# The third K quarter of an MLP's second product: plain instead of Strassen, with activations split as they are made

## The chip, the cores and the metric

The kernel runs on one core of a Trainium2 chip. The time is that of one execution on the device in microseconds (us); where several runs are given, their median counts. A core has a matrix engine (TensorE, PE in the rows; its weight loads are shown apart as PEld), a vector engine (DVE), a scalar engine (ACT), GpSimd (POOL, which here does little but issue DMAs that add to what is in their destination) and SyncE (SP, which issues the other DMAs). Each engine works through its own queue in order; semaphores tie the queues to each other. Matmuls write into PSUM, eight banks of 128 x 512 fp32; DVE and ACT take the results from there.

## What is computed

One layer of a diffusion backbone for 512 tokens of width 1024 with a context of 256 tokens. The change lies in its last part, the MLP:

```python
def mlp(s, shift, scale_m):
    hm = rms_norm(s, g_norm2) * (1.0 + scale_m) + shift
    return jnp.square(jax.nn.relu(hm @ w_mlp1)) @ w_mlp2

x_new = x.astype(jnp.float32) + gt1 * merge(y_attn, o_dl, dz, ga, gd)
x_new = x_new + gt2 * mlp(x_new, sh2, sc2)
```

`w_mlp1` is 1024 x 4096 and `w_mlp2` 4096 x 1024. What stands ahead of it (modulated norms, one wide projection, windowed attention, a gated delta rule in chunks, the branch projections) is the same before and after, but for the order in which its instructions are issued.

## The kernel before

**Numbers.** Every large product is made of three matmuls of a reduced fp32 format: an operand is split into a high part (a rounding copy on ACT, line 231) and a low part (the difference, on DVE, line 232; the helper `split` holds both), and high x high, high x low and low x high are summed in PSUM.

**The MLP by quarters.** The hidden width of 4096 is worked off in four quarters (`hf` 0 to 3) of 1024. In each quarter the first product makes `hb`, the squared activations, 1024 hidden rows by 512 tokens; the second product takes `hb` as the stationary operand and the quarter's rows of `w_mlp2` as the moving one. In quarter 0 the first product is plain (`wload` and `mm3`, lines 335 to 339). In the others the class `Pair` makes two blocks of 128 hidden rows at a time by Strassen's scheme with seven half-size products (line 1619, 128x256), four pairs a quarter. At a pair's end its sums go through Relu (line 1654) and Square (line 1656) on ACT into `hb`.

**The second product.** In quarters 0 to 2 the class `Down` does it by Strassen's scheme as well: seven products of half size in K, tokens and columns. Its activation sides are made from quarters of `hb` by `left` (sums on lines 1783 and 1786, then a split), its weight sides by DMAs that add one weight block to another in SBUF (line 1733, on POOL's queue) and a split. Matmuls are on lines 1807 to 1809. Each of the seven results has a running total over the quarters in SBUF, `accs_`: written by ACT in quarter 0, added to by DVE (line 1828) in quarters 1 and 2. In quarter 3 the class `Flat` does the product plainly: for each half `n` of the 1024 columns it holds four banks, one for each 128 tokens, and sums four pieces of K (256 rows each) into them (lines 1876 to 1878). Its `left` splits each piece of `hb` behind the pairs.

**The totals.** The generator `gather` turns the seven totals into the four blocks of the result: seven DMAs that add one total to another (line 1894), a gate row made by eight transposes (line 1898), four multiplications by the gate (line 1908), and eight DMAs that add the residual parked in the output tensor (line 1910). It advances among the pairs of quarter 3 (`GAT`). `Flat` then multiplies its own PSUM by the gate (line 1885), adds it (line 1887) and stores the result (line 1888).

**Loads for the next quarter.** `Down.run` starts the next quarter's first weights behind its fifth to seventh product (`LOADS`).

**What sets the order.** The code records all instructions first. `arrange` then issues them by a list scheduler with a cost model: on each engine the ready instruction with the lowest rank goes next. The rank is the place at which the code recorded it, changed by the table `SHIFTS`: an entry `(engine, first, end, places)` adds `places` to the rank of the recorded instructions `first` to `end` of that engine (0 PE, 1 DVE, 2 ACT; -1 all). So the table moves instructions on each engine, but the data they need stays the same. SBUF is one arena that is handed out in the order of recording; an instruction that writes a place again waits for the earlier readers.

Of the kernel before, what the change touches and what calls it, by code (L numbers as in the profile page):

```python
# [42 lines left out]
OUT = 4, 128, 1024  # L43
LAHEAD = 1
GAT = 0, 2
LOADS = (4, 5), (4, 5, 6)
P = 128
D = 1024
# [73 lines left out]
def tile_layer(ctx: ExitStack, tc: tile.TileContext, I: dict, out: bass.AP, dbg=None):  # L122
    nc = tc.nc
# [1450 lines left out]
    class Pair:  # L1574
# [67 lines left out]
        def second(self):  # L1642

            w, z = bank(), bank()
            o = self.o
            self.prod(w[:, :256], "12", "21")
            V.tensor_tensor(o[:, :256], self.u[:, :256], w[:, :256], op=ALU.add)
            w.free()
            self.u.free()
            self.prod(z[:, :256], "22", "T4")  # L1650
            self.prod(z[:, 256:], "S4", "22")
            V.tensor_tensor(o[:, 256:768], o[:, 256:768], z.ap, op=ALU.add)
            z.free()
            A.activation(o.ap, o.ap, AF.Relu)
            at = self.f % FT * 512
            A.activation(hb[:, at:at + 1024], o.ap, AF.Square)
            o.free()

    def combos():
# [175 lines left out]
    class Flat:  # L1835


        def __init__(self, hf):

            self.hf, self.src, self.parts = hf, I["wm2"][hf], []  # L1840
            self.made = self.pieces()
            self.ready = [next(self.made) for _ in range(2)]

# [9 lines left out]
                        split(e, hi, lo)  # L1853
                        yield [r32(b.rearrange("p (k c) -> p k c", k=2)) for b in (hi, lo)]

        def left(self):

            at = len(self.parts) * 1024
            bs = [alloc(1024), alloc(1024)]
            split(hb[:, at:at + 1024], *[b.ap for b in bs])  # L1860
            self.parts.append([r32(b.ap.rearrange("p (k t) -> p k t", k=2)) for b in bs])

        def run(self):

            self.ready.append(next(self.made))
            for n in range(2):
                z = [bank() for _ in range(4)]
                for p in range(4):
                    if len(self.parts) < 4:
                        self.left()  # L1870
                    hi, lo = self.parts[p]
                    wh, wl = self.ready.pop(0)
                    for tt, zz in enumerate(z):
                        c = slice(tt * P, tt * P + P)
                        for k in range(2):
                            PE.matmul(zz.ap, hi[:, k, c], wh[:, k], start=(p == k == 0), stop=False)  # L1876
                            PE.matmul(zz.ap, hi[:, k, c], wl[:, k], start=False, stop=False)  # L1877
                            PE.matmul(zz.ap, lo[:, k, c], wh[:, k], start=False, stop=(p == 3 and k == 1))  # L1878
                    m = next(self.made, None)
                    if m:  # L1880
                        self.ready.append(m)
                for tt, zz in enumerate(z):
                    cols, r = slice(n * 512, n * 512 + 512), tt % 2 * 512
                    y, t = alloc(512), ends[f"{1 + tt // 2}{1 + n}"][:, r:r + 512]
                    V.tensor_tensor(y.ap, zz.ap, grow[0][:, cols], op=ALU.mult)
                    zz.free()
                    V.tensor_tensor(t, t, y.ap, op=(ALU.add, ALU.subtract)[n])
                    nc.sync.dma_start(out=out[tt][:, cols], in_=t)
                    y.free()

    def gather():

# [21 lines left out]
            accs_.pop(w).free()  # L1914
        yield

    ends = {}
    grow = []
    FT = 8
    pairs = [[Pair(hf * FT + f) for f in range(0, FT, 2)] if hf else [] for hf in range(4)]  # L1920
# [3 lines left out]
    for hf in range(4):  # L1924
# [17 lines left out]
        if hf == 0:  # L1942
            for _ in late:
                pass
            scr_[0].free()
        ps_ = pairs[hf]
        for i, p_ in enumerate(ps_):
            p_.first()
            if i:
                p_.load2()  # L1950
            if i + 1 < len(ps_):
                p_.second()
            if i + 2 < len(ps_):
                ps_[i + 2].load1()
            if hf == 3 and i in GAT:
                next(last)
            if i == 2:
                down = (Flat if hf == 3 else Down)(hf)
                down.left()
        if hf:  # L1960
            ps_[-1].second()
        if hf == 3:
            for _ in last:
                pass
        down.run()
# [143 lines left out]
class Lists:  # L2109
# [177 lines left out]


SHIFTS = (
# [21 lines left out]
)  # L2311


# [120 lines left out]
```

## Time and profile before

| what | value |
|---|---|
| runs | 850.16, 851.46, 853.50 us, median 851.46 us |
| the profiled execution | 848.21 us |
| its span, from the first to the last instruction | 846.4 us |
| granted clock of TensorE | 0.999 of full speed |
| DMA moved | 127.31 MB, mean 150 GB/s |
| first Strassen product of the MLP's second product, on TensorE | from 556 us |
| last quarter's plain product, on TensorE | about 795 to 842 us |

Rows of groups read: line, engine, operation, what it writes and reads by the program's names (`m` is any buffer of the arena, `wh` and `wl` the high and low weights, `wr` raw weights), shape and count, then busy time in us, mean ns of one, and the engine's idle time just before, with what ended it. TensorE is the busiest engine by far in every stage; DVE comes next, and in the MLP it is busy for most of the time as well. Matmuls overlap in the pipeline, so the mean of one is longer than the step from one to the next.

### The profile page before, as it was taken

Reading aid. Unit: us, or ns where it says so; the run is one execution under the profiler, and the core shown is the slowest. Engines: PE = TensorE matmul, PEld = TensorE weight load, DVE = VectorE, ACT = ScalarE, POOL = GpSimd, SP = SyncE. Lnnn points to the kernel's source line nnn. Section 1 sums busy time; section 2 is a strip of 40 time slices with the busy share of each in tenths; the row PEclk is TensorE's granted clock in tenths of the full one; section 3 lists DMA queues with packets and bytes.
Section 4 is the critical chain, followed back from the end, with each engine's and each line's share of the span. In section 5 each row is a group of like instructions: output and inputs, shape, how many; then the busy total and the mean of one; then the engine's idle time right before and its main releaser. Section 6 shows DMA issues by size and latency. Waiting matters only on the chain.

```text
span 846.4 us, 18086 instructions
## 1 busy us (share of the span) xinstructions
PE 833.7 (98%) x7464; PEld 698.4 (83%) x7464; DVE 699.2 (83%) x1153; ACT 534.2 (63%) x920; POOL 60.3 (7%) x81
## 2 busy tenths in 40 slices
PE   8999999999999999999999999999999999999997
PEld 5688778887877778787778899888998899889986
DVE  5875999988779998868849879798689988989853
ACT  5568785487769896587754345398557447646520
POOL 0000011010000002000000000110011001111300
PEclk9999999999999999999999999999999999999999
DMA  9924365543221237643116755959259636998271
GB/s 367 369 76 100 76 151 124 124 85 70 38 38 31 62 116 243 213 141 103 41 41 246 241 161 190 312 131 264 95 157 194 169 129 162 187 269 229 35 190 50
DMA packets 38178, 127.31 MB, mean 150 GB/s; under 512 B 4688, under 2 KB 5200, under 8 KB 38096
## 3 DMA queue, kind: packets, MB, share of 16 engines
q1 hardware_dynamic: 30176, 99.43, 34.3%
q0 software_dynamic: 7920, 26.74, 18.6%
q8 instruction: 58, 0.95, 0.5%
q14 instruction: 24, 0.20, 0.1%
HBM read 118.29 MB, written 4.19 MB: 145 GB/s over the span
## 4 chain that ended last, share of the span: by engine, by line
PE 92%; DMA 5%; ACT 1%; DVE 1%; SPq 0%; issue 0%; ACTq 0%
PE banks L1619 14%; PE banks L1155 14%; PE banks L335 9%; PE banks L337 9%; PE banks L339 9%; PE banks L1809 4%; PE banks L1807 4%; PE banks L1808 4%; PE banks L1250 3%; PE banks L1201 3%; DMA m<-in_wada 2%; PE banks L732 2%; PE banks L1876 2%; PE banks L1878 2%; PE banks L1877 2%; DMA wr<-in_win 1%
## 5 line engine op out<-in xcount | busy, mean ns | idle before, releaser
L1619 PE MATMUL banks<-m,m 128*128 128x256 f32 x1008 | 126.2, 284 | 0.7 <-ACT m L231 0.7
L1619 PEld LDWEIGHTS banks<-m,m 128*128 128x128 f32 x1008 | 123.6, 192 | 2.9 <-ACT m L231 1.6
L231 ACT ACTIVATE m<-m 128x512 fp32r<-128x512 f32 (+2 forms) x123 | 90.9, 761 | 52.7 <-PE banks L1808 8.6
L232 DVE TENSOR_TENSOR m<-m,m 128x512 fp32r<-128x512 f32 (+2 forms) x123 | 103.0, 854 | 15.2 <-ACT m L231 12.9
L335 PE MATMUL banks<-m,wh 128*128 128x512 f32 (+1 forms) x312 | 112.1, 363 | 0.0
L337 PE MATMUL banks<-m,wh 128*128 128x512 f32 (+1 forms) x312 | 110.2, 355 | 0.0
L339 PE MATMUL banks<-m,wl 128*128 128x512 f32 (+1 forms) x312 | 109.6, 354 | 0.0
L1155 PE MATMUL banks<-m,wh 128*128 128x512 f32 x320 | 104.4, 401 | 1.3 <-ACT m L189 1.3
L299 ACT ACTIVATE wh<-wr 128x1024 fp32r<-128x1024 f32 (+1 forms) x60 | 56.6, 944 | 47.8 <-DMA wr<-in_wout 13.9
L1155 PEld LDWEIGHTS banks<-m,wh 128*128 128x128 f32 x320 | 59.2, 188 | 14.3 <-ACT m L189 1.8
L335 PEld LDWEIGHTS banks<-m,wh 128*128 128x128 f32 x312 | 58.9, 189 | 8.5 <-issue 0.5
L337 PEld LDWEIGHTS banks<-m,wh 128*128 128x128 f32 x312 | 59.0, 189 | 8.2 <-issue 0.5
L339 PEld LDWEIGHTS banks<-m,wl 128*128 128x128 f32 x312 | 58.9, 189 | 8.1 <-DVE wl L304 0.2
L1807 PE MATMUL banks<-wh,m 128*128 128x512 f32 x168 | 65.4, 392 | 0.0
L1808 PE MATMUL banks<-wl,m 128*128 128x512 f32 x168 | 65.2, 390 | 0.0
L1155 PE MATMUL banks<-m,wl 128*128 128x512 f32 x160 | 64.4, 404 | 0.4 <-DVE wl L304 0.4
L1809 PE MATMUL banks<-wh,m 128*128 128x512 f32 x168 | 64.4, 391 | 0.0
L304 DVE TENSOR_TENSOR wl<-wr,wh 128x1024 fp32r<-128x1024 f32 (+1 forms) x44 | 45.1, 1024 | 13.3 <-ACT wh L299 13.2
L335 PE MATMUL banks<-m,m 128*128 128x256 f32 (+1 forms) x136 | 45.6, 341 | 0.6 <-ACT m L344 0.5
L231 ACT ACTIVATE wh<-m 128x1024 fp32r<-128x1024 f32 x30 | 31.6, 1055 | 22.8 <-DMA m<-in_wm 15.5
L1733 POOL DMA_DIRECT2D m<-in_wm x24 | 20.8, 920 | 348.9 <-PE banks L339 167.2
L337 PE MATMUL banks<-m,m 128*128 128x256 f32 (+1 forms) x136 | 44.9, 337 | 0.1
(298 smaller groups left out, 1814.1 us busy)
## 6 DMA issues: line engine op xcount, KB each, us to landing
m<-in_wada SPq DMA_DIRECT2D x48, 512.0 KB, 5.0
wr<-in_win SPq DMA_DIRECT2D x38, 512.0 KB, 3.8
m<-in_wm SPq DMA_DIRECT2D x36, 512.0 KB, 4.9
wr<-in_wm SPq DMA_DIRECT2D x28, 512.0 KB, 4.5
m<-in_wm POOLq DMA_DIRECT2D x24, 512.0 KB, 7.6
wl<-in_win POOLq DMA_DIRECT2D x16, 512.0 KB, 6.0
m<-in_xT SPq DMA_DIRECT2D x8, 512.0 KB, 4.8
wr<-in_wbr SPq DMA_DIRECT2D x16, 256.0 KB, 2.6
```

The lines of the kernel that those rows point to most:

```text
L231: A.activation(r32(hi), src, AF.Copy)
L232: (eng or V).tensor_tensor(r32(lo), src, hi, op=ALU.subtract)
L299: upper[0] = A.activation(r32(hi), raw, AF.Copy)
L304: V.tensor_tensor(r32(lo), raw, hi, op=ALU.subtract)
L335: PE.matmul(acc, w[0][:, k, :], xhi, start=(start and i == 0), stop=False)
L337: r = PE.matmul(acc, w[0][:, k, :], xlo, start=False, stop=(end and w[1] is None))
L339: r = PE.matmul(acc, w[1][:, k, :], xhi, start=False, stop=end)
L1155: PE.matmul(acc.ap, w[x][:, k, :], hx[k][y], start=(k == p == 0), stop=(k == KT - 1 and p == 2))
L1619: PE.matmul(dst, r32(self.w[w][i][:, k * P:(k + 1) * P]), xs7[x][k][j], start=(n == 0), stop=(n == 11))
L1807: PE.matmul(zz, hi[:, kk, ts_], wh[:, k], start=(kk == 0), stop=False)
L1808: PE.matmul(zz, hi[:, kk, ts_], wl[:, k], start=False, stop=False)
L1809: PE.matmul(zz, lo[:, kk, ts_], wh[:, k], start=False, stop=(kk == 3))
```

## The change

The third quarter's second product becomes plain as well, so the class `Flat` now serves quarters 2 and 3 (`FLAT = 2`), and `Down` quarters 0 and 1. In those two quarters each pair splits its squares at once: Square in place, then the high copy into `hb` and the low part into a buffer of its own in the list `lows`; `Flat.left` is gone. At quarter 2 `hb` is given back and taken anew from the arena. `gather`, which needs the Strassen totals, now runs among the pairs of quarter 2, and `Flat` in quarter 2 adds its results to the gated blocks without storing them. `Flat.run` starts the next quarter's loads behind the first three K pieces of its second column half (`FLOADS`). The table `SHIFTS` is replaced by another of the same kind.

```diff
+FLAT = 2
+FLOADS = 4, 5, 6
...
             A.activation(o.ap, o.ap, AF.Relu)
             at = self.f % FT * 512
-            A.activation(hb[:, at:at + 1024], o.ap, AF.Square)
+            if self.f < FLAT * FT:
+                A.activation(hb[:, at:at + 1024], o.ap, AF.Square)
+            else:
+                A.activation(o.ap, o.ap, AF.Square)
+                lows.append(alloc(1024))
+                split(o.ap, hb[:, at:at + 1024], lows[-1].ap)
...
-            self.hf, self.src, self.parts = hf, I["wm2"][hf], []
+            self.hf, self.src = hf, I["wm2"][hf]
+            if hf < 3:
+                self.loads = [pairs[hf + 1][0].load1, pairs[hf + 1][0].load2, pairs[hf + 1][1].load1]
...
-        def left(self):
-
-            at = len(self.parts) * 1024
-            bs = [alloc(1024), alloc(1024)]
-            split(hb[:, at:at + 1024], *[b.ap for b in bs])
-            self.parts.append([r32(b.ap.rearrange("p (k t) -> p k t", k=2)) for b in bs])
...
-                    if len(self.parts) < 4:
-                        self.left()
-                    hi, lo = self.parts[p]
+                    hi, lo = (r32(ap.rearrange("p (k t) -> p k t", k=2)) for ap in (hb[:, p * 1024:p * 1024 + 1024], lows[p].ap))
...
+                    if n:
+                        lows[p].free()
+                    if self.hf < 3 and 4 * n + p in FLOADS:
+                        self.loads.pop(0)()
...
-                    nc.sync.dma_start(out=out[tt][:, cols], in_=t)
+                    if self.hf == 3:
+                        nc.sync.dma_start(out=out[tt][:, cols], in_=t)
...
+        if hf == FLAT:
+            hb.free()
+            hb = alloc(FT * 512, True)
...
-            if hf == 3 and i in GAT:
+            if hf == FLAT and i in GAT:
                 next(last)
             if i == 2:
-                down = (Flat if hf == 3 else Down)(hf)
-                down.left()
+                down = (Flat if hf >= FLAT else Down)(hf)
+                if hf < FLAT:
+                    down.left()
...
 SHIFTS = (
-    (-1, 3553, 4764, 98), (-1, 3512, 3594, 1006), (-1, 7403, 7446, -155), (-1, 1987, 1996, 101), (0, 2046, 2292, -17),
+    (0, 3509, 4763, 98), (0, 1987, 1996, 132), (0, 2046, 2346, -13), (-1, 6045, 6078, -107), (-1, 2025, 2189, -11),
```

In the order rows below, the line numbers of the changed kernel are two higher than before as far as line 1655; its plain product keeps lines 1876 to 1878. First TensorE where the third quarter's pairs end and its second product begins (`m_6546` and the like are pair operands, `m_8067` and `m_8068` the high and low of Strassen's first activation side). Before:

```order
L1619 MATMUL banks<-m_6546,m_8129 128x256 x2
L1619 MATMUL banks<-m_6546,m_8130 128x256
L1807 MATMUL banks<-wh_8058,m_8067 128x512
L1808 MATMUL banks<-wl_8059,m_8067 128x512
L1809 MATMUL banks<-wh_8058,m_8068 128x512
```

and of the change (`m_7698` is the new `hb`, `m_7793` the low half of its first piece):

```order
L1621 MATMUL banks<-m_6546,m_8158 128x256 x2
L1621 MATMUL banks<-m_6546,m_8159 128x256
L1876 MATMUL banks<-wh_8090,m_7698 128x512
L1877 MATMUL banks<-wl_8091,m_7698 128x512
L1878 MATMUL banks<-wh_8090,m_7793 128x512
```

The Strassen product's rows are replaced by the plain product's at the same place; 18 of the plain ones already stand further up among the pairs.

Second ACT at the last two pairs of that quarter (`m_7941`, `m_8071` before and `m_7955`, `m_8100` after are the pairs' sums, `m_6265` the old `hb`). Before:

```order
L1654 ACTIVATE m_7941<-m_7941 128x1024
L1656 ACTIVATE m_6265<-m_7941 128x1024
L231 ACTIVATE m_8067<-m_6265 128x1024
L231 ACTIVATE wh_8063<-m_8050 128x1024
L231 ACTIVATE m_8183<-m_8185 128x1024
L231 ACTIVATE wh_8179<-m_8052 128x1024
L1654 ACTIVATE m_8071<-m_8071 128x1024
L231 ACTIVATE wh_8202<-m_8054 128x1024
L1656 ACTIVATE m_6265<-m_8071 128x1024
```

and of the change:

```order
L1656 ACTIVATE m_7955<-m_7955 128x1024
L1661 ACTIVATE m_7955<-m_7955 128x1024
L1632 ACTIVATE m_8101<-banks 128x512
L233 ACTIVATE m_7698<-m_7955 128x1024
L233 ACTIVATE m_8427<-m_8379 128x512
L233 ACTIVATE m_8382<-m_8378 128x512
L233 ACTIVATE m_8423<-m_8378 128x512
L1656 ACTIVATE m_8100<-m_8100 128x1024
L1661 ACTIVATE m_8100<-m_8100 128x1024
L233 ACTIVATE wh_8242<-wr_8240 128x1024
L233 ACTIVATE m_7698<-m_8100 128x1024
```

The copies that made Strassen's sides (`m_8067`, `m_8183`) are gone; relu, square and the high copy of a pair stand close together, with a weight copy and the next quarter's pair operands between them.

Third TensorE in the attention part, at the last projection product ahead of a wait for ACT (`st_2604` is a set of softmax sums, `wh_2426` and `wh_2596` the weights of two projection blocks). Before:

```order
L722 MATMUL banks<-m_2725,m_562 128x512
L1155 MATMUL banks<-m_136,wh_2426 128x512
L1155 MATMUL banks<-m_136,wl_2427 128x512
L753 MATMUL banks<-c_ident,st_2604 128x128
L1155 MATMUL banks<-m_136,wh_2596 128x512 x2
```

and of the change:

```order
L724 MATMUL banks<-m_2725,m_562 128x512
L1157 MATMUL banks<-m_136,wh_2426 128x512
L1157 MATMUL banks<-m_136,wl_2427 128x512
L755 MATMUL banks<-c_ident,st_2604 128x128 x2
L1157 MATMUL banks<-m_136,wh_2596 128x512 x2
```

One of the set's transposes, which stood further up, has moved down to this place.

More of the change, by code (lines that the diff above doesn't have):

```diff
@@ L1887, in run @@
                     V.tensor_tensor(t, t, y.ap, op=(ALU.add, ALU.subtract)[n])
-                    nc.sync.dma_start(out=out[tt][:, cols], in_=t)
+                    if self.hf == 3:
+                        nc.sync.dma_start(out=out[tt][:, cols], in_=t)
                     y.free()
+            lows.clear()
     def gather():
@@ L1915, in gather @@
         yield
-    ends = {}
+    ends, lows = {}, []
     grow = []
@@ L1954, in tile_layer @@
                 ps_[i + 2].load1()
-            if hf == 3 and i in GAT:
+            if hf == FLAT and i in GAT:
                 next(last)
             if i == 2:
-                down = (Flat if hf == 3 else Down)(hf)
-                down.left()
+                down = (Flat if hf >= FLAT else Down)(hf)
+                if hf < FLAT:
+                    down.left()
         if hf:
             ps_[-1].second()
-        if hf == 3:
+        if hf == FLAT:
             for _ in last:
```

38 rows, old and new, of the table SHIFTS are left out of this document.

## The prediction

> **What bounds the kernel now.** I read the page's head and its chain first, then TensorE's own rate by windows, then what TensorE waited for.
>
> ```profile
> span 846.4 us, 18086 instructions
> PE 833.7 (98%) x7464; PEld 698.4 (83%) x7464; DVE 699.2 (83%) x1153; ACT 534.2 (63%) x920; POOL 60.3 (7%) x81
> ...
> PE 92%; DMA 5%; ACT 1%; DVE 1%; SPq 0%; issue 0%; ACTq 0%
> ```
>
> TensorE is busy for 98% of the span and is 92% of the chain that ended last. Busy time overlaps itself, since matmuls are pipelined, so I look at the step from one to the next. The first row is the pairs' group on the page (count, busy, mean ns, idle before). The columns of a window are its length, then busy time and count (x) of PE, weight loads, DVE, ACT, POOL, then clock and DMA.
>
> ```profile
> L1619 PE MATMUL banks<-m,m 128*128 128x256 f32 x1008 | 126.2, 284 | 0.7 <-ACT m L231 0.7
> ...
> 680.00:720.50 40.50, 40.50 (x328) 39.99 (x327) 35.38 (x55) 24.67 (x33) 3.48 (x4) 1.00 0.50 131
> 720.50:761.40 40.90, 40.90 (x202) 34.43 (x201) 38.29 (x39) 23.53 (x27) 6.93 (x8) 1.00 0.95 229
> 761.40:797.00 35.60, 35.60 (x293) 35.01 (x292) 33.65 (x53) 23.53 (x33) 2.61 (x3) 1.00 0.50 139
> ...
> 604.00:634.00 30.00, 30.00 (x252) 30.00 (x251) 26.07 (x40) 18.36 (x25) 1.72 (x2) 1.00 0.40 125
> ...
> 800.00:840.00 40.00, 40.00 (x178) 33.10 (x178) 19.83 (x25) 8.39 (x8) 4.41 (x5) 1.00 0.51 128
> ...
> 730.00:744.00 14.00, 14.00 (x64) 11.58 (x63) 14.00 (x14) 8.52 (x9) 2.59 (x3) 1.00 0.86 208
> ```
>
> The first three windows are, roughly, the third quarter's pairs, its Strassen product, and the fourth quarter's pairs. The window 800 to 840 holds nothing on TensorE but the plain product of the last quarter. A matmul lasts 0.39 us there (the row of line 1878 further down), so the 178 began within 40.39 us: **0.227 us a step**. In the Strassen product (730 to 744) it is 14.39 / 64 = 0.225, so one 128x512 matmul costs the same in either form. A pair's 128x256 matmuls last 0.284 us and step at 30.28 / 252 = 0.120 (604 to 634, only pairs). The clock is 1.00 throughout.
>
> ```profile
> PE banks L1155 <- ACT m L189: 1.3, 2, 0.7
> PE banks L276 <- ACT m L271: 1.2, 1, 1.2
> PE banks L237 <- DVE ones L202: 1.1, 1, 1.1
> PE banks L732 <- DVE m L747: 0.8, 1, 0.8
> PE banks L1619 <- ACT m L231: 0.7, 1, 0.7
> PE banks L256 <- ACT m L189: 0.6, 1, 0.6
> PE banks L335 <- ACT m L344: 0.5, 1, 0.5
> PE banks L1155 <- DVE wl L304: 0.4, 1, 0.4
> PE banks L256 <- DVE modS L286: 0.3, 1, 0.3
> PE banks L407 <- DVE m L406: 0.3, 1, 0.3
> PE banks L256 <- DMA m<-in_wada: 0.2, 1, 0.2
> PE banks L681 <- ACT m L189: 0.2, 1, 0.2
> ```
>
> This is all that TensorE waited for (total, times, longest): 7.6 us. Behind 440 us there is one wait alone, 0.7 us on line 1619, and it stands where the first quarter's product meets the second quarter's pairs, ahead of anything the change rewrites. The waits on lines 276, 237, 335, 407 and 256, 4.2 us, belong to the first 40 us; the other 2.7 us lie between. So **the MLP's time is TensorE's instruction stream and nothing else**.
>
> **The change, part by part.** *Matmuls.* The Strassen product issues 7 products x 2 pieces x 2 row tiles x 2 x 3 = 168 matmuls of 128x512; the plain one 2 column halves x 4 pieces x 4 row tiles x 2 x 3 = 192. The code fixes both counts, so 24 more at 0.227 us: **+5.4 us**, all of it on the path. The bounds are 24 x 0.225 = 5.4 from the neighbouring window and, if the matmuls somehow ran like the half-size ones, 24 x 0.120 = 2.9. I take 5.4, the row of the very code that is used again.
>
> The Trainium skill bears on this (TensorE: Matmul & The Clock Gate, "Back-to-back issue gap"): it puts a sustained stream of weight loads and 512-column matmuls at about 131 ns each, and by that the term would be an estimated 24 x 0.131 = 3.1 us. Both windows disagree with it by 70%. So the rule is only a rival, below.
>
> *Vector and scalar work.* Counted over the two orders, the third quarter loses 13 DVE instructions that write 128x1024 (6 weight splits, 3 activation splits, 4 Strassen sums) and the 7 additions of line 1828, and gains 8 + 8 of 128x512 (lines 1885, 1887).
>
> ```profile
> L231 ACT ACTIVATE wh<-m 128x1024 fp32r<-128x1024 f32 x30 | 31.6, 1055 | 22.8 <-DMA m<-in_wm 15.5
> ...
> L232 DVE TENSOR_TENSOR wl<-m,wh 128x1024 fp32r<-128x1024 f32 x30 | 36.6, 1219 | 4.0 <-ACT wh L231 3.8
> ...
> L1828 DVE TENSOR_TENSOR m<-m,banks 128x1024 f32<-128x1024 f32 x14 | 17.0, 1214 | 2.9 <-PE banks L1809 2.9
> ...
> L1885 DVE TENSOR_TENSOR m<-banks,m x8: 679/686/692, 816.8 to 841.7; 128x512 f32<-128x512 f32 x8
> ```
>
> That is -13 x 1.22 - 7 x 1.21 + 16 x 0.69 = -13 us of DVE (line 1887 taken as line 1885), and ACT loses nine copies of 1.06 us. POOL loses 8 accumulating loads; SP's count stays (4 fewer raw and 4 fewer direct loads for the Strassen product, 8 for the plain one). Value: **nothing**. All of it runs beside TensorE, which waits for none of it in this quarter; even the MLP's single wait would give only 0.7 us. Below nothing: DVE could get crowded where work moves *in*. Into the third quarter's pairs come 4 low halves and the 4 gate products of line 1908, 8 x 1.22 = 9.8 us, and about 3 us of Strassen preparation goes out: 35.4 + 9.8 - 3 = 42 us of DVE beside 40.5 us of pairs and the 18 plain matmuls that now stand among them (4.1 us). That fits by 2 us. The fourth quarter's pairs in 761 to 797 already have DVE at 33.65 of 35.6 with no wait. So I put 0 to +3 us on it and take 0.
>
> *The chain behind the last pair.* Relu, square, copy and low half now follow each other; in the third quarter only the fourth K piece of the plain product needs the last pair's. After the last pair's matmul 78 of that half's matmuls remain, 54 ahead of the fourth piece: 54 x 0.227 = 12.3 us. The chain takes DVE 0.69, ACT 3 x 1.06, DVE 1.22 and a weight copy between, about 6 us. It is hidden; without that cover it would cost up to 6 us once.
>
> *Totals behind the second quarter.* POOL's seven additions and eight loads move one quarter forward with their rank in the queue kept.
>
> ```profile
> L1910 POOL DMA_DIRECT2D m<-out x8: 867/2018/3163, 797.3 to 801.2; - x8
> ...
> DMA to landing us min/median/max: 4.1/8.5/12.2
> ```
>
> Now the last is issued at 801.2 and lands at most 12.2 us on, 813.4; the first use is 816.8 or later (line 1885's row). After the change line 1908 stands among the second and third pairs on DVE, earlier against the same use than now, when it comes at the pairs' end, so the margin of 3 us or more grows. Cost 0. The fourth quarter's DVE is freed of it, and nobody waited there.
>
> *The end.* Only the last rows count, since the output store itself is unchanged.
>
> ```profile
> 841.30 0.39 PE L1878 MATMUL banks<-wh,m 128*128 128x512 f32 x1
> 841.73 0.69 DVE L1885 TENSOR_TENSOR m<-banks,m 128x512 f32<-128x512 f32 x1 [2.66 <-PE banks L1878]
> 842.45 0.69 DVE L1887 TENSOR_TENSOR m<-m,m 128x512 f32<-128x512 f32 x1
> 843.17 0.33 SPq L1888 DMA_DIRECT2D out<-m  x1
> ```
>
> One multiply, one addition and one store follow the last matmul. In the new order the last row tile's own 12 matmuls (2.7 us) come alone behind the others, where it was 18; the tile ahead of it needs 2 x 0.69 = 1.4 us, so the tail stays at one tile's. Cost 0.
>
> *The new shifts* move rows all through the program, also in the 556 us ahead of the first Strassen product. Two in five of TensorE's rows there change place, but the changes between whole-array and part-array matmuls stay at 110, and POOL's and SP's queues keep their order. The larger wait on line 189 shows what that can bring:
>
> ```profile
> 264.32 0.39 PE L1155 MATMUL banks<-m,wl 128*128 128x512 f32 x1
> 264.55 0.27 PE L753 MATMUL banks<-c_ident,st 128*128 128x128 f32 x1
> 265.56 0.73 PE L1155 MATMUL banks<-m,wh 128*128 128x512 f32 x2 [0.74 <-ACT m L189]
> ```
>
> One more transpose now stands in front of the waiting matmul, which wins at most that transpose's 0.27 us; the waiting matmul itself still stands right behind the same product, whose bank ACT must read first. The rows at the other waits (lines 732, 681 and the other two of line 1155) keep the instruction that ends them. In the first 40 us some 128x32 matmuls of line 256 go about one microsecond ahead of ready work; one of them waited 0.3 us for line 286, which also moves ahead by two on DVE. I take 0 for the order, with bounds: at best the 2.7 us between 40 and 440 and the MLP's 0.7 us all go (-3.4), at worst about as much is made anew (+3).
>
> **Sum.** **+5.4 us**. The profiled execution took 848.21 us (its span 846.4 and 1.8 around it), which would become 853.6. The three runs' median is 851.46, 3.25 above that one execution, and I carry the same addition: **856.9 us**. Half a per cent, about what a measurement of this kernel can tell from no change, is 4.3 us: 847.2 to 855.7. The forecast lies outside by only 1.2 us.
>
> **Rivals.** *The new order pays it back (not slower).* One mechanism: shifted rows put ready matmuls of lines 1155 and 721 into the waits between 40 and 440 us. Price: up to 3.4 us, so 851.46 + 5.4 - 3.4 = 853.5 us. It decides from 5.4 - 4.3 = 1.1 us of recovered waiting on. For it: all of these waits have other matmuls of the same stage close by. Against it: at those places both orders look alike. To get *faster* by over 0.5% the order would have to win 9.7 us, more than the 7.6 us of all waits in the trace, so it must also shorten the small gaps that no wait is named for.
>
> *A fuller DVE turns into a wait in the third quarter's pairs.* Price up to 3 us, 859.9 us. For it: 42 us of work in 44.6. Against it: 95% in the fourth quarter now, with no wait.
>
> *The added matmuls step faster than those of today.* From rows the floor is the half-size step: 24 x 0.120 = 2.9, 851.46 + 2.9 = 854.4 us, no change by the bound. Against it: 0.225 and 0.227 in two windows with either product. The Trainium skill's sustained 131 ns, on the page named above, would be this case; the trace speaks against it.
>
> **How the numbers follow.** Forecast 0.54; order pays back 0.28; a new DVE wait 0.11; a faster step 0.03; the order wins far more 0.04. The forecast's own spread of some 2 us about 856.9 crosses 855.7: I count 0.07 of its 0.54 as "same" and all of the DVE case as slower. Slower 0.47 + 0.11 = 0.58; same 0.07 + 0.28 + 0.03 = 0.38; faster 0.04. The range takes in the payback case with its own spread and the DVE case: 851.5 to 860.
>
> **What would show it.** Right: the plain matmuls of both quarters at 0.227 us a step, 24 more, the third quarter's pairs and product 5 us longer together, no wait on TensorE there, and the first Strassen product starting at the same time as now. Wrong: that product starting over 1.1 us earlier (the order); a wait of line 1619 or 1876 for DVE or ACT in the third quarter (crowding); a wait of line 1887 for POOL's loads; or a last store later than 5 us behind the last matmul.

## The result, and the profile after

The change made the kernel **slower by 0.7%**. In the comparison that judges it, five runs of the changed kernel gave a median of 857.07 us (855.38 to 857.88) and five of the kernel before 852.54 us (850.16 to 854.05): ratio 1.0072, 95% interval 1.0053 to 1.0090. A second comparison, made with the experiments, gave 855.68 us against 849.54 us: 1.0062 (1.0045 to 1.0078). By these ratios the change costs 6.1 and 5.3 us; 5.4 us and 856.9 us had been forecast. The ratios are not the quotients of the medians beside them: those are 1.0053 (4.5 us) and 1.0072 (6.1 us), so the cost is known to about a microsecond.

A warning for whoever subtracts the two traces: the profiled execution of before took 848.21 us, 4.3 us less than the median of its five runs, while that of after took 857.07 us, its median exactly. The difference of the two traces is therefore 8.9 us, of which about 3 to 4 us are the choice of executions. All that follows uses several executions of each order.

The head and the chain of waits of after's page (busy us, share of the span, instructions):

```profile
span 855.3 us, 18102 instructions
PE 840.9 (98%) x7488; PEld 703.2 (82%) x7488; DVE 686.0 (80%) x1149; ACT 525.3 (61%) x911; POOL 53.4 (6%) x73
...
PE 84%; DMA 7%; DVE 6%; ACT 2%; issue 1%; SPq 0%; ACTq 0%; DVEq 0%
```

24 matmuls more, DVE 13 us less, ACT 9 us less and POOL 8 instructions less, as counted beforehand; TensorE is still busy for 98% and bounds the kernel. Its share of the chain is lower than before (84% for 92%), since the chain follows the three waits shown below (2.7 us in all) back through splits and loads for some 87 us; in a second trace of the same kernel, without these waits, it is 94%. So that share is no measure of lost time. The group of the plain product's first line, and the window of after that lies wholly in the third quarter's plain product (length, then busy and count of PE, weight loads, DVE, ACT, POOL, then clock, DMA share, GB/s):

```profile
L1876 PE MATMUL banks<-wh,m 128*128 128x512 f32 x128 | 49.9, 390 | 0.0
...
730.00:744.00 14.00, 14.00 (x63) 11.62 (x62) 10.88 (x14) 7.47 (x9) 0.00 (x0) 1.00 0.22 77
```

The line serves both quarters now (128 where it had 64), a matmul lasts 0.39 us as before and (14.00 + 0.39) / 63 = 0.228 us is the step. In the same window DMA's share fell from 0.86 to 0.22. None of that is worth time, since TensorE did not wait there before either.

What TensorE waited for in after, behind 440 us (total, times, longest; the other rows of this view lie ahead of the MLP):

```profile
PE banks L1621 <- ACT m L233: 1.5, 1, 1.5
...
PE banks L1814 <- ACT wh L233: 0.8, 1, 0.8
...
PE banks L341 <- DVE wl L306: 0.4, 1, 0.4
```

Two of these are new and stand where the third quarter begins and in its pairs, at 667 us (line 1814, among the last matmuls of the second quarter's Strassen product) and at 696 us (line 1621), where the forecast had none. The wait of before at 586 us is gone.

### The profile page after: what moved, and what is told of

The parts are those of the page before. It is cut to its first block, busy times and chain, and to the rows that moved or that the text cites. A ratio compares the mean times of both kernels' runs of the same rounds, so it can differ in the third digit from the quotient of the medians.

```text
span 855.3 us, 18102 instructions
## 1 busy us (share of the span) xinstructions
PE 840.9 (98%) x7488; PEld 703.2 (82%) x7488; DVE 686.0 (80%) x1149; ACT 525.3 (61%) x911; POOL 53.4 (6%) x73
## 4 chain that ended last, share of the span: by engine, by line
PE 84%; DMA 7%; DVE 6%; ACT 2%; issue 1%; SPq 0%; ACTq 0%; DVEq 0%
PE banks L1157 14%; PE banks L1621 13%; PE banks L337 8%; PE banks L339 8%; PE banks L341 7%; PE banks L1876 3%; PE banks L1877 3%; PE banks L1878 3%; PE banks L1252 3%; PE banks L1203 3%; DMA m<-in_wada 3%; PE banks L1815 2%; PE banks L1816 2%; PE banks L1814 2%; PE banks L734 2%; DMA wr<-in_win 1%
## 5 line engine op out<-in xcount | busy, mean ns | idle before, releaser
L233 ACT ACTIVATE m<-m 128x512 fp32r<-128x512 f32 (+2 forms) x120 | 87.4, 754 | 59.7 <-DVE m L1612 11.4
L234 DVE TENSOR_TENSOR m<-m,m 128x512 fp32r<-128x512 f32 (+2 forms) x120 | 98.8, 848 | 14.7 <-ACT m L233 12.6
L233 ACT ACTIVATE wh<-wr 128x1024 fp32r<-128x1024 f32 x24 | 25.4, 1057 | 42.3 <-PE banks L1878 31.0
L1876 PE MATMUL banks<-wh,m 128*128 128x512 f32 x128 | 49.9, 390 | 0.0
L1877 PE MATMUL banks<-wl,m 128*128 128x512 f32 x128 | 49.9, 389 | 0.0
L1878 PE MATMUL banks<-wh,m 128*128 128x512 f32 x128 | 49.8, 389 | 0.0
L337 PE MATMUL banks<-m,m 128*128 128x512 f32 (+1 forms) x136 | 45.6, 341 | 1.0 <-ACT m L301 0.7
L520 DVE SCALAR_TENSOR_TENSOR m<-m,m 128x1024 f32<-128x1024 f32 x32 | 39.0, 1222 | 9.3 <-DMA m<-in_wada 9.3
L339 PE MATMUL banks<-m,m 128*128 128x256 f32 (+1 forms) x136 | 45.5, 339 | 0.0
```

The source lines that it names most:

```text
L233: A.activation(r32(hi), src, AF.Copy)
L234: (eng or V).tensor_tensor(r32(lo), src, hi, op=ALU.subtract)
L337: PE.matmul(acc, w[0][:, k, :], xhi, start=(start and i == 0), stop=False)
L339: r = PE.matmul(acc, w[0][:, k, :], xlo, start=False, stop=(end and w[1] is None))
```

## Experiments

Each ratio is against the kernel before on the same chip. Stretches are read from the start of TensorE's rows in the traces: "MLP" is the time from the first matmul of the first Strassen product (of the MLP's second product) to the last matmul of all.

| run | time, us (median) | ratio (95%) | first Strassen product, us | MLP, us | waits behind 440 us |
|---|---|---|---|---|---|
| before, first trace | 852.54 | | 555.73 | 285.57 | 586 |
| before, second trace | 851.48 (one run) | | 556.99 | 287.59 | 587, 647, 651, 789 |
| after, first trace | 857.07 | 1.0072 (1.0053 to 1.0090) | 557.13 | 293.07 | 496, 667, 696 |
| after, second trace | 855.68 | 1.0062 (1.0045 to 1.0078) | 556.32 | 289.91 | none |
| early order of before | 854.40 | 1.0055 (1.0042 to 1.0068) | 556.52 | 289.89 | 496 |
| before with early order of after | 850.52 | 1.0011 (1.0001 to 1.0021) | 556.71 | 285.41 | 587 |
| 24 fewer, first half | 852.80 | 1.0035 (1.0016 to 1.0054) | 557.33 | 287.55 | 695, 712, 731, 733 |
| 12 fewer, first half | 852.72 | 1.0026 (1.0011 to 1.0042) | 556.82 | 289.18 | 695, 707 |
| 24 fewer, second half | 850.00 | 1.0007 (0.9995 to 1.0018) | 558.40 | 284.95 | 497, 777 |
| small totals | 855.16 | 1.0069 (1.0048 to 1.0090) | 557.29 | 290.28 | none |
| fourth quarter alone plain | 851.13 | 1.0015 (1.0003 to 1.0027) | 556.73 | 287.92 | 587, 769, 787, 789 |
| before with new order of the first quarters | 854.57 | 1.0050 (1.0031 to 1.0069) | 556.37 | 292.38 | five from 634 to 660, three later |

The last column says where a matmul followed the one before it over 0.25 us later than the usual step (the time in us; 587 is the wait of before at 586).

### Both kernels once more

No edit. The kernel before:

> The kernel before, unchanged, profiled a second time: its first profiled execution (848.21 us) lay 4.3 us below the median of its five runs, so single traces cannot simply be subtracted. If the spread is a matter of single executions at one and the same instruction order, the first Strassen product should start anywhere within about 1.5 us of 555.7 us here, and the 0.9 us stall near 586 us may or may not be there. If the early order is what the change costs at its start (+1.4 us at that point in the two first traces), this trace starts that product at 555.7 +- 0.3 us and every trace of the changed kernel at 557.1 +- 0.3.

The kernel after:

> The changed kernel, unchanged. Time against before: 1.0055 to 1.009 (+4.5 to +8 us). If the two new waits on TensorE (about 1.0 us at 667 us on line 1814, about 1.7 us at 696 us on line 1621) belong to the order, they stand in this trace too, at the same instructions and with 0.8 us or more each; if they were chance of the one execution, at least one is missing or under 0.3 us.

One order spreads: the first Strassen product started at 555.73 and at 556.99 us in the two traces of before, and at 557.13 and 556.32 us in those of after. The sharper form of the expectation (one fixed time for each order) fell at once. All waits that the second trace of after names, in the view's order:

```profile
PE banks L278 <- ACT m L273: 1.2, 1, 1.2
PE banks L1157 <- ACT m L191: 1.2, 2, 0.6
PE banks L239 <- DVE ones L204: 1.1, 1, 1.1
PE banks L734 <- DVE m L749: 0.8, 1, 0.8
PE banks L258 <- ACT m L191: 0.6, 1, 0.6
PE banks L337 <- ACT m L301: 0.4, 2, 0.3
PE banks L1157 <- DVE wl L306: 0.4, 1, 0.4
PE banks L258 <- DVE modS L288: 0.3, 1, 0.3
PE banks L258 <- DMA m<-in_wada: 0.3, 1, 0.3
PE banks L1013 <- issue: 0.2, 1, 0.2
PE banks L683 <- ACT m L191: 0.2, 1, 0.2
```

No row of lines 1621, 1814 or 1876: the two new waits of the first trace are not fixed parts of the new order. The quickest traces of both kernels can now be set side by side: MLP 285.57 and 289.91 us, **4.3 us** apart.

### The early order and the MLP apart

The changed kernel, with the entries of before in `SHIFTS` for what is recorded ahead of the MLP (indices under 5740) and its own behind:

```diff
-    (0, 3509, 4763, 98), (0, 1987, 1996, 132),
...
+    (-1, 3553, 4764, 98), (-1, 3512, 3594, 1006),
...
     (-1, 6045, 6078, -107), (1, 5742, 6785, -6835),
...
```

> The changed kernel's MLP (its last 1730 rows on TensorE as in the changed kernel) behind the order of before in everything ahead of the MLP (the first 3008 rows on TensorE as before). Theory C (the early order costs nothing by itself, the 1.4 us at the first Strassen product in the two first traces was chance of the two executions): first Strassen product between 555.5 and 557.3 us, time against before as the changed kernel's, 1.005 to 1.008. Rival (the new early order costs 0.7 to 1.4 us): 1.0045 to 1.006, first product at 555.7 to 556.5. Rival (the new early order gains 2 to 3 us, which the MLP eats): 1.009 to 1.010.

And the kernel before with the new entries under 5740 and its own behind:

> The other half: the MLP of before (last 1722 rows on TensorE) behind the early order of the changed kernel. Theory C: 0.999 to 1.0015 of before, as many matmuls as before. Rival (early order costs): 1.001 to 1.002. Rival (early order gains): 0.9965 to 0.998. Together with the run of the early order of before, the two ratios less one should add up to that of the whole change.

Both ratios, 1.0055 and 1.0011, lie in the range of the theory that the early order costs nothing and in that of its rival, so the two do not decide it. The two parts add up: 0.55% for the MLP and 0.11% for the early order make 0.66%, between the 0.72% and the 0.62% of the whole. So **the MLP costs 4.7 us (3.6 to 5.8) and the early order 0.9 us (0.1 to 1.8)**. The traces point the same way on the second: with the early order of before the first Strassen product starts at 555.73, 556.99, 556.73, 556.52 and 556.37 us, 556.5 on average; with the new one at 557.13, 556.32, 556.71, 557.29, 557.33, 558.40 and 556.82, 557.1 on average, which is 0.7 us more where one order alone spreads by 1.3 us. The early order gains nothing; that it costs something is barely shown, since no cost at all lies just outside the interval.

### 24 of the added matmuls taken out, twice

In `Flat.run`, for quarter 2, the product of the activations' low half and the weights' high half is left out for three of four K pieces, first in the first column half, with the ranks of all other instructions kept:

```diff
+                            if self.hf == 2 and n == 0 and p < 3:
...
+                                continue
                             PE.matmul(zz.ap, lo[:, k, c], wh[:, k], start=False, stop=(p == 3 and k == 1))
```

> The changed kernel with 24 of the 192 matmuls of the third quarter's plain product left out (low halves of the activations by high halves of the weights, first column half, first three K pieces), everything else and its order as in the changed kernel: as many matmuls as the Strassen product had. Theory A (each added matmul costs its full step): 24 x 0.227 = 5.4 us less than the changed kernel, so 0.9998 to 1.003 of before. Rival (they step at 0.131 us): 3.1 us less. Rival (the stage waits for operands, so that matmuls are cover): under 1.5 us less.

Only 0.27% went, 2.3 us, which is less than Theory A's 5.4 and its first rival's 3.1; in the traces the MLP got 289.91 - 287.55 = 2.4 us shorter. The rest came back as waits, which the waits of TensorE name, line 1881 being the low x high matmul here:

```profile
PE banks L1876 <- ACT m L233: 1.2, 1, 1.2
...
PE banks L1881 <- DVE m L234: 0.7, 1, 0.7
```

The gaps between matmuls there, less the usual step, are 1.4 and 0.9 us, and two smaller ones at 695 and 712 us 0.3 each, so 5.4 - 2.9 = 2.5 us is what the rows leave. The stretch in the timeline (start, us, engine, line, operation; in brackets the idle time before and what ended it), DVE, then ACT, then TensorE:

```profile
726.39 0.69 DVE L234 TENSOR_TENSOR m<-m,m 128x512 fp32r<-128x512 f32 x1 [1.90 <-ACT m L233]
727.00 0.68 DVE L1654 TENSOR_TENSOR m<-m,banks 128x512 f32<-128x512 f32 x1
...
732.79 1.22 DVE L234 TENSOR_TENSOR m<-m,m 128x1024 fp32r<-128x1024 f32 x1
```

```profile
725.72 1.15 ACT L233 ACTIVATE m<-m 128x512 fp32r<-128x512 f32 x2 [1.96 <-DMA m<-in_wm]
727.71 1.06 ACT L1656 ACTIVATE m<-m 128x1024 f32<-128x1024 f32 x1 [0.84 <-DVE m L1654]
...
731.52 1.04 ACT L233 ACTIVATE m<-m 128x1024 fp32r<-128x1024 f32 x1
```

```profile
731.00 0.39 PE L1877 MATMUL banks<-wl,m 128*128 128x512 f32 x1
732.62 0.50 PE L1876 MATMUL banks<-wh,m 128*128 128x512 f32 x1 [1.23 <-ACT m L233]
732.95 0.40 PE L1877 MATMUL banks<-wl,m 128*128 128x512 f32 x1
734.06 0.50 PE L1881 MATMUL banks<-wh,m 128*128 128x512 f32 x1 [0.72 <-DVE m L234]
```

This is the chain behind the last pair, whose last matmul ended at 724.1 us. Its addition on line 1654 began only at 727.00, since DVE, in order, stood before a split whose copy waited for a load (725.72 on ACT). Relu, square, the high copy (to 732.56) and the low half (to 734.01) follow, with two weight copies between. The fourth K piece starts when the high copy ends, and its low half's first matmul when the low half does. In the changed kernel 54 matmuls stand between the last pair's matmul and the fourth piece and cover this chain; here the trace has 32 (7.3 us; the next expectation counts 30). So the experiment removed cover and matmuls at once, and the second version leaves the cover whole (`n == 1` in place of `n == 0`):

> The changed kernel again with 24 matmuls of the third quarter's plain product left out (low halves of the activations by high halves of the weights, first three K pieces), but from the second column half. In the run of the first half 24 x 0.227 = 5.4 us of steps went and 2.3 us came back as two waits at 731 and 733 us, on the first matmuls of the fourth K piece. Theory A with the chain behind the last pair (Relu, square, copy, low half: 7 to 10 us from the last pair's matmul, hidden by 54 matmuls = 12.3 us in the changed kernel, by 30 = 6.9 us there): this time the 54 stand, so no wait on the fourth K piece and the full 5.4 us go: 0.999 to 1.002 of before. Rival (the third quarter is paced by something else, loads or copies of weights, so that matmuls there are partly cover): only about 3 us go, 1.002 to 1.005, with waits of 2 us in the second column half or the pairs behind it.

Now it is level with before, at 1.0007, and the MLP takes 284.95 us, 5.0 us less than after's quickest, with one gap of 0.45 us at 777 us (0.3 us of it in the row of TensorE's waits below). The issue order moved a little too, and two of the fourth quarter's loads went out 20 us earlier (59 us behind the third quarter's first pair matmul, where after's second trace has 79), but the third quarter's stretch runs at the steps alone. From its first pair matmul to its product's last, after's second trace has 238 matmuls of 128x512 and 344 of 128x256: 238 x 0.227 + 344 x 0.120 = 95.3 us, and it took 95.27. Here they are 214 and 344, 89.9 us, and it took 89.81. **The 24 matmuls are the MLP's cost**, 5.4 us of steps, and nothing paces the third quarter in their place as long as the chain is covered.

```profile
PE banks L1621 <- ACT m L233: 0.3, 1, 0.3
```

Between the two, 12 matmuls left out of the first half (the same edit with `and k == 0`):

> The changed kernel with 12 matmuls left out ahead of the fourth K piece in the third quarter's first column half (low halves of the activations by high halves of the weights, first of the two 128-row slices of the first three K pieces), so that 42 x 0.227 = 9.5 us of matmuls stand over the chain behind the last pair, between the 12.3 us of the changed kernel (no wait) and the 6.8 us of the run with 24 left out (2.3 us of waits). Theory A with the chain at 7 to 10 us: 2.7 us less than the changed kernel and a wait on the fourth K piece of 0 to 0.5 us, so 1.002 to 1.0045 of before. Rival (chain of 6 us as predicted, the waits with 24 left out came from late loads alone): no wait at all, same time.

1.0026, 0.36% below after's ratio of 1.0062 in another comparison. Its trace has no wait on the fourth K piece, so 9.5 us of cover were still enough, and 7.3 us were not. It has another wait, on line 1621 at 695 us, the one that after's first trace showed, and a smaller one at 707 us; without these two gaps, 1.5 and 0.4 us, its MLP is 289.18 - 1.9 = 287.3 us, 2.6 us less than after's quickest, where 12 steps are 2.7.

### The totals on 16 of their 1024 columns

That wait stands some 28 us behind the third quarter's first pair matmuls, while POOL's transfers of the totals, which the change moved here, are under way:

```diff
-            G.dma_start(out=accs_[x].ap, in_=accs_[y].ap, accum_op=ALU.add)
+            G.dma_start(out=accs_[x][:, :16], in_=accs_[y][:, :16], accum_op=ALU.add)
```

> The changed kernel with the seven accumulating transfers of the totals on 16 columns in place of their whole width (most of the totals' sum is left out), same instructions in the same order. Theory B (these transfers share the DMA engines with the third quarter's weight loads, which then land late): the waits at 667 us (line 1814) and 696 us (line 1621) shrink to under 0.3 us, the loads of line 1594 issued near 683 land in 3 to 5 us instead of 9 to 10, and the time falls by 1.5 to 2.7 us against the changed kernel. Rival (the waits come from the order of the loads alone): both waits stay, time within 0.7 us of the changed kernel.

The time did not move (1.0069); the fall of 1.5 to 2.7 us did not come. But the second trace of after had shown meanwhile that the waits need not be there, so this run could gain little. Its order is also not quite that of the changed kernel, which the expectation takes it to be: in the third quarter splits on ACT and DVE and one weight load stand in other places, and 13 plain matmuls in place of 18 stand among the pairs. What it does show is the loads. The DMA issues of two 512 KB loads of line 1594 (1592 before), from issue to landing in us (the median of the two), for before, after's first and second trace, the run with small totals, and that with 12 fewer matmuls:

```profile
m<-in_wm SPq DMA_DIRECT2D x2, 512.0 KB, 3.5
```

```profile
m<-in_wm SPq DMA_DIRECT2D x2, 512.0 KB, 9.4
```

```profile
m<-in_wm SPq DMA_DIRECT2D x2, 512.0 KB, 6.7
```

```profile
m<-in_wm SPq DMA_DIRECT2D x2, 512.0 KB, 5.0
```

```profile
m<-in_wm SPq DMA_DIRECT2D x2, 512.0 KB, 9.4
```

With the whole totals the loads take 6.7 to 9.4 us, with small ones 5.0. The 3.5 us of before are not quite the same thing: its two loads were issued 6.1 us apart, those of the others 1.3. The two traces that waited for over 1 us are those with 9.4; the other four with whole totals have 6.7 to 8.1. It holds in all seven traces with this third quarter, with the landing of the first of the two loads counted from the third quarter's first pair matmul (the 337th of 1008):

| trace | landing after that matmul, us | idle on line 1621 near 695 us, us |
|---|---|---|
| small totals | 19.1 | none |
| after, second | 19.6 | none |
| 24 fewer, second half | 20.1 | none |
| early order of before | 20.9 | none |
| 24 fewer, first half | 21.1 | 0.1 |
| 12 fewer | 22.5 | 1.3 |
| after, first | 23.0 | 1.5 |

How the load reaches TensorE, in after's first trace: ACT stood idle for it, DVE for ACT's copy, and a later copy on ACT then came too late for the matmul (timelines of ACT, DVE, ACT and TensorE).

```profile
691.73 1.15 ACT L233 ACTIVATE m<-m 128x512 fp32r<-128x512 f32 x2 [3.42 <-DMA m<-in_wm]
692.40 1.90 DVE L234 TENSOR_TENSOR m<-m,m 128x512 fp32r<-128x512 f32 x3 [1.30 <-ACT m L233]
...
697.11 1.06 ACT L233 ACTIVATE m<-m 128x1024 fp32r<-128x1024 f32 x1 [0.23 <-DVE m L1601]
```

```profile
698.22 0.98 PE L1621 MATMUL banks<-m,m 128*128 128x256 f32 x6 [1.54 <-ACT m L233]
```

So the loads are slower where the totals run beside them, and have some 21 us of slack; past it a wait of up to 1.5 us follows, in two of the six executions with whole totals (0.1 us in a third). In the kernel before, which moves the totals in its fourth quarter, two loads of line 1592 issued beside them at 749.9 and 766.3 us took 6.7 and 5.9 us; but one at 723.3, ahead of the first of these transfers (741.6 us), took 8.0, so loads can be slow without them as well. That the totals' volume is the cause of the slow loads rests on one run (5.0 us, at another order) against six; that it costs time was not seen directly, since the run that took it away is compared with a kernel that mostly does not wait. What makes one execution's loads slower than another's at one order stays open, and so does the wait at 667 us, which stands in after's first trace alone.

### What is left when the third quarter is Strassen's again

The changed code with `FLAT = 3` and the shifts of before: only the fourth quarter is plain, and its activations are split as they are made.

```diff
-FLAT = 2
+FLAT = 3
```

> The changed code with its plain quarters set to the fourth alone (third by the Strassen product again, totals in the fourth quarter) and the shifts of before: what is left of the change is that the fourth quarter's activations are split as they are made, in place. As many matmuls as before (7464). Theory A (the added matmuls are the whole cost): 0.999 to 1.0015. Rival (the split as made, on the way of the pairs, costs by itself): 1.002 or more, with a wait of line 1621 or 1876 on ACT or DVE in the fourth quarter.

1.0015 (1.0003 to 1.0027): nearly all of the cost is gone with the plain third quarter. The rest, 1.3 us (0.3 to 2.3), is at the edge of what Theory A allows, and the rival's sign is there in part, so what it comes from is not clear. The trace has 2.1 us of waits of the pairs on ACT:

```profile
PE banks L1621 <- ACT m L233: 2.1, 3, 1.1
```

One is the old one at 587 us, the others are in the fourth quarter, where ACT came to a weight copy whose load was late (1.06 us idle for it at 768.72 us) with the pair's copy queued behind.

### A piece of the new order in the kernel before

In all four traces with the MLP order of before, TensorE waits near 586 us, as here in the first trace of before; in none of the seven with the changed kernel's does it.

```profile
586.20 0.39 PE L1808 MATMUL banks<-wl,m 128*128 128x512 f32 x1
587.33 0.39 PE L1619 MATMUL banks<-m,m 128*128 128x256 f32 x1 [0.74 <-ACT m L231]
```

1.13 us lie between the two starts, 0.9 more than a step. To have that without the matmuls, the kernel before got the new entries of `SHIFTS` for the indices 5740 to 6200 alone:

```diff
-    (-1, 6044, 6077, -106), (1, 5748, 5839, -1941),
+    (-1, 6045, 6078, -107), (1, 5742, 6200, -6835), (-1, 6143, 6195, -21), (0, 5899, 5917, -49), (0, 5926, 6155, 22),
```

> The kernel before, with the changed kernel's order only between the first quarter's product and the middle of the second quarter's pairs (TensorE's first 3008 rows and its last 704 as before): no plain third quarter, no other part of the change. Theory D (the 0.7 to 1.0 us wait of the pairs on ACT near 586 us, in all four traces with the old order of the MLP and in none of the six with the new one, is a matter of the order, and its going paid back 0.9 us of the added 5.4): that wait is gone, 0.9985 to 0.9995 of before. Rival (it goes and something behind it takes the time): wait gone, 0.9995 to 1.001. Rival (chance): the wait is there.

The wait near 586 is gone, as in every trace with the new order at this place, so it belongs to the order. But the kernel is 0.5% slower than before, more than the rival had allowed. Among its waits are new ones where the new order meets the old, in the second quarter's Strassen product and pairs:

```profile
PE banks L1807 <- ACT wh L231: 1.2, 1, 1.2
...
PE banks L1809 <- DVE m L232: 0.8, 1, 0.8
...
PE banks L1808 <- DVE wl L232: 0.6, 2, 0.4
...
PE banks L1619 <- DVE m L232: 0.6, 2, 0.4
...
PE banks L1807 <- ACT m L231: 0.5, 1, 0.5
```

At the same matmul counts its MLP takes 292.38 us in this trace where 285.41 are possible; by the ratio a seam in the order costs 4.2 us (2.6 to 5.9), nearly as much as the change itself. No run beat the kernel before.

## Why the prediction was right, step by step

- **Matmuls, +5.4 us: right.** 24 more at the step of 0.227 to 0.228 us; without them the kernel is level with before. The third quarter's pairs and product were to get 5 us longer together: from the first pair matmul to the product's last it is 94.57 us before and 95.27 in after's second trace, but the stretch of before holds 42 matmuls of the fourth quarter's pairs, 5.0 us, so they got 5.7 us longer. The Trainium skill's sustained 131 ns (TensorE: Matmul & The Clock Gate, "Back-to-back issue gap") would make an estimated 3.1 us of it; the step in both plain products and the 5.0 us that the MLP lost without them speak against it at this kernel's number format.
- **Vector and scalar work, nothing: right.** 13 us of DVE and 9 us of ACT went, and the fourth quarter's pairs have much lighter DVE, for no gain. The crowding in the third quarter was rightly sized, at 42 of 44.6 us or 94%, though its window left out the pairs' first 14 us; it did not bind: in the second trace of after, DVE is busy for 53.20 of the 56 us around those pairs, 95%, with no wait there.

```profile
667.00:723.00 56.00, 56.00 (x409) 53.08 (x408) 53.20 (x75) 32.59 (x45) 12.30 (x14) 1.00 0.88 218
```

- **The chain behind the last pair, hidden: right, though mis-sized.** It had been put at 6 us. From the end of the last pair's matmul to the end of the low half it takes 7.2 us in the second trace of after (722.97 to 730.15) and 9.9 us with 24 fewer matmuls, where DVE stood before a late load. What it left out is the queue ahead of it on DVE, an engine that works in order. With 12.3 us of cover neither matters; with 7.3 us of cover the longer one left waits of 2.3 us.
- **Totals behind the second quarter, cost 0: the step that failed.** It asked whether the totals come in time for their use, and they do: in after's first trace the last transfer is issued at 718.5 us and lands at most 7.9 us on, and the first addition that needs one starts at 743.3. It did not ask whom their transfers hold up. In the row above the DMA share is 0.88, where the third quarter's pairs of before had 0.50, and the loads beside them take up to 9.4 us, where small totals leave 5.0. The price, as far as these transfers are the cause, is 1.3 to 1.5 us in two of six executions; so the sign "no wait on TensorE there" failed in the very trace shown with the result. A wait of the pairs on ACT in the third quarter was also the sign set for a crowded DVE; but ACT had idled 3.42 us for the load, and DVE 1.30 us for ACT's copy, so the late load began it.
- **The end, 0: right.** One multiply, one addition and the store follow the last matmul, at the same distance: the addition starts 1.15 us behind that matmul's start, as before.

```profile
850.20 0.39 PE L1878 MATMUL banks<-wh,m 128*128 128x512 f32 x1
850.63 0.69 DVE L1889 TENSOR_TENSOR m<-banks,m 128x512 f32<-128x512 f32 x1 [1.30 <-PE banks L1878]
851.35 0.69 DVE L1891 TENSOR_TENSOR m<-m,m 128x512 f32<-128x512 f32 x1
```

- **The new shifts, 0: right in sum, by two terms that cancel.** Ahead of the MLP they cost 0.9 us (0.1 to 1.8) where the rival of an order that pays back hoped for a gain of up to 2.7 us there. In the MLP they took away the wait near 586 us, 0.9 us, which the prediction had as a bound and not as its value. The MLP's 4.3 to 4.5 us between quiet traces is 5.4 less this 0.9. The bound of +3 us for waits made anew was a guess, and another order of the same kernel, the seam, went beyond it with 4.2 us.

The sum of what was found: 5.4 - 0.9 + 0.9, and some 0.5 us for the loads held up (three waits of 1.5, 1.3 and 0.1 us over six executions). That is 5.9 us, between the 5.3 and the 6.1 us of the two ratios. That the forecast of 856.9 us lies 0.2 us from the median of 857.07 is luck beyond that: it was built on a median of before of 851.46 us, which was 852.54 in the comparison that judges it and 849.54 in the next.

## What to carry to other kernels

Where one engine is busy for 98% and steps evenly, count its instructions first: work taken from the other engines is worth nothing there, and a scheme that saves matmuls keeps its value until it makes that engine wait. When a transfer is moved, ask not only whether it lands in time, but which loads run beside it at the new place and how much slack they have. And profile both kernels twice before believing a wait: one that stands in one of two traces of the same order is not a property of the order.

## What had not been expected of the hardware

- At one and the same order, two 512 KB loads beside the seven adding transfers took 6.7 us in one execution and 9.4 in another. With the seven transfers cut to 16 of 1024 columns, at a somewhat different order, they took 5.0 us; two loads 6 us apart with no such transfers beside them, in the kernel before, took 3.5 us.
- Executions of one kernel on one chip spread over 3.6 us (before, 848.48 to 852.05 us in 13 runs), and the start of one stage at the same order by 1.3 us, with a granted clock of 0.99 or more throughout.
